# Both parts of x in one product: a two-layer decoder trunk in split fp32 on one core

## The chip, the cores and the metric

The kernel runs on one core of one Trainium2 chip. The metric is device time in microseconds (us), from one launch that computes the whole reference; three runs of the kernel before gave a median of 913.07 us (912.96 to 913.5).

The engines are named as the profile names them: PE is the matrix engine (its weight loads are a row of their own, PEld), DVE the vector engine, ACT the activation engine, POOL the general engine, SP the engine that issues most DMAs.

## The reference, cut to what matters

Two layers, 256 positions, 1024 channels, all in float32. Each layer normalises a mixer's sum and then an MLP's sum:

```
h = layer_norm(x)
for l in range(2):
    h = layer_norm(ALPHA*h + mixer(h))
    gate, val = split(h @ w_up)                 # 2 x 2816 columns
    gate = causal_conv3(gate) + conv_b
    h = layer_norm(ALPHA*h + (silu(gate) * val) @ w_down)
```

The mixer projects h into three groups of heads: A (forgetting attention, `aq`, `ak`, `av`), B (sparse attention with an index of the 64 best keys) and C (differential attention); the three results are gated, added and projected. The units whose products this change rearranges are those of `aq` and `ak`, which the kernel keeps transposed as `qaT` and `kaT`, and the up-projection of the MLP.

## The kernel before, in words

**Split fp32.** Every product is done three times in the matrix engine's fast fp32 form: a value is stored as a high part (`hi`, rounded to that form) and a low part (`lo`, the remainder), and the sum hi·hi + lo·hi + hi·lo is accumulated in a PSUM bank of 128 x 512 floats. Weights come from memory in one flat stream in the order of use (`stream_plan`, L77; class `Stream`, L112): a DMA on SP's queue brings a chunk of 1024 floats per partition into one of 7 `raw` buffers; `Stream.split` (L146) makes an item `hl` of 128 x 2 x 512 in one of 16 buffers, the high part with an ACT copy, the low part with a DVE subtraction (POOL's for some at the start), and then issues the next chunk's DMA on SP.

**Activations.** The normalised h, transposed, is a pair of tiles `hTh` and `hTl` (`new_hT`, L531), each 8 blocks of 128 channels by 256 positions.

**Two kinds of units.** `unit_x` (L668) and `unit_x_tbfirst` (L680) have h as the stationary operand and 512 columns of weights as the moving one, once for each block of 128 positions (`tb`). `unit_w` (L695) has the weights stationary and the 256 positions moving, so that the result comes out transposed. It is used four times for `qaT` and `kaT` (two in each layer) and for pairs 1 to 10 of the MLP in each layer (a pair is 256 gate and 256 value columns; pair 0 goes through `unit_x`'s form and is transposed). For each block k and each of four groups of 128 output columns it issues three products of 128 x 256: wh·xh, wl·xh, wh·xl.

**MLP.** The banks G and V of a pair are handed to `task_act` (L1250): two ACT operations read G (scale and bias of the convolution), four DVE operations read G again (the convolution's other taps), ACT does the silu, DVE multiplies by V, and the result is split into the `act` tile. After the unit of pair j come the 24 products of `down` of pair j-1 into the four `dacc` banks; the products of the last two pairs come at the end, ordered by output half `nh` first and then by pair d, once for each `tb`. `ln_half` (L535) adds the residual and takes statistics of one half.

**The first norm.** `first_norm` (L599), once for each block of 128 positions: h is normalised without gain, transposed by PE into two banks (one for each half q), DVE multiplies each bank by the gain and adds the bias in place (two operations of 128 x 512), and `split_out` (L571) makes the high part with one ACT copy and the low part with one DVE subtraction. `spins(n)` issues n products of no use while PE has nothing to do.

**Order.** Engines run their instructions in the order in which the program emits them. `Clocks` (L201) estimates when each would end, generators (`Tasks`, L282) are advanced at every `T.tick()`, and `refill` (L182) emits splits when the lead in weights is low or DVE has time. `W.hold` stops splits while a norm's chain runs. Banks come from two pools of four: `acc` for the units with h stationary and for `qaT` and `kaT`, `att` for everything else.

Of the kernel before, what the change touches and what calls it, by code (L numbers as in the profile page):

```python
# [76 lines left out]
def stream_plan():  # L77
# [4 lines left out]
    def add(n, kts, cols=512, k0=0):  # L82
        step = 2 if cols <= 512 else 1
        for k in range(k0, k0 + kts, step):
            plan.append((n, k, step, cols))
# [3 lines left out]
    for n in ("biq", "cq", "ck", "cv", "aq", "ak", "av"):  # L89
        add(n, 8)  # L90
    for b in (1, 0):
        for nh in range(2):
            add(f"gate{b}{nh}", 8)
            add(f"br{b}{nh}", 4)
# [10 lines left out]
    for j in range(NPAIR):  # L105
        add(f"up{j}", 8)
# [5 lines left out]
class Stream:  # L112


    def __init__(self, nc, ve, sc, clocks, flat, raw_pool, hl_pool, plan):
# [6 lines left out]
        for (_, _, kts, cols) in plan:  # L122
# [4 lines left out]
            w = 512 if cols >= 512 else cols  # L127
# [68 lines left out]
def part(x):  # L196

    return x.name + "low" if x.name[:2] == "hl" and x.offset % 1024 >= 512 else x.name
# [126 lines left out]
def tile_hybrid(ctx: ExitStack, tc: tile.TileContext, a: dict, out: bass.AP):  # L325
# [273 lines left out]
    def first_norm(tb, st, hT, flag):  # L599
# [13 lines left out]
        for q in range(2):  # L613
# [4 lines left out]
            v = bk.rearrange("p (k t) -> p k t", k=4)  # L618
            for i, f in enumerate((ALU.mult, ALU.add)):
                ve.tensor_tensor(v, v, gb[:, i, 4 * q:4 * q + 4].unsqueeze(2).broadcast_to([P, 4, P]), f)  # L620
        spins((9, 5)[tb])
        if tb:
            att_free(warm)
        for q, bk in enumerate(bks):
            split_out(hT[0][:, 4 * q:4 * q + 4, tb * P:(tb + 1) * P],
                      hT[1][:, 4 * q:4 * q + 4, tb * P:(tb + 1) * P],
                      bk.rearrange("p (k t) -> p k t", k=4))
            att_free(bk)
            if not tb and not q:
                W.split(gp)  # L630
# [64 lines left out]
    def unit_w(hT, bks):  # L695

        for k in range(KD):
            w = W.take()
            for i in range(4):
                o = bks[i // 2][:, (i % 2) * 256:(i % 2) * 256 + 256]  # L700
                l = w[:, :, i * P:(i + 1) * P]
                first = k == 0 and i % 2 == 0
                mm(o, l[:, 0, :], hT[0][:, k, :], first, False)
                mm(o, l[:, 1, :], hT[0][:, k, :], False, False)
                mm(o, l[:, 0, :], hT[1][:, k, :], False, k == KD - 1)
                if i % 2:
                    T.tick()
# [17 lines left out]
    def layer(l, hT, hflag):  # L725
# [524 lines left out]
        def task_act(j, G, V):  # L1250
# [10 lines left out]
            att_free(G)  # L1261
# [3 lines left out]
            att_free(V)  # L1265
# [17 lines left out]
        for j in range(NPAIR):  # L1283
# [3 lines left out]
            G, V = get_att(), get_att()  # L1287
            unit_w(hT1, [G, V])
            T.add(task_act(j, G, V))
# [18 lines left out]
        for tb in range(2):  # L1308
            ts = slice(tb * P, (tb + 1) * P)
            st = small([P, 2, 6], "bst")  # L1310
            for i, (nh, c0, c1) in enumerate(PIECES):
                W.hold = W.hold or nh == 1
                for d in (NPAIR - 2, NPAIR - 1):
                    T.until(lambda: d in acts)
                    for f in range(2):
                        w = ws[d, f, nh][:, :, c0:c1]
                        mm3(dacc[nh][tb][:, c0:c1], acts[d][:, 0, f, ts], acts[d][:, 1, f, ts],
                            w[:, 0, :], w[:, 1, :], False, d == NPAIR - 1 and f == 1)
                        if tb and c1 == 512:
                            W.free()  # L1320
                        if True:
                            T.tick()
                if not (tb and nh and l < DEPTH - 1):
                    ln_half(tb, nh, st, dacc[nh][tb], (c0, c1), i)
# [105 lines left out]
```

## Time and profile before

| | |
|---|---|
| median of 3 runs | 913.07 us (912.96 to 913.5) |
| the profiled execution: time, span | 913.03 us, 911.2 us |
| granted clock of PE, mean | 0.997 |
| PE busy | 898.0 us, 99% of the span, 5334 products |
| PEld busy | 786.7 us, 86% |
| DVE busy | 652.1 us, 72%, 1272 instructions |
| ACT busy | 512.1 us, 56%, 1008 instructions |
| POOL busy | 46.4 us, 5% |
| memory read | 159.47 MB, mean 177 GB/s |

The profile is one execution. Its span runs from the first to the last instruction; the 1.8 us between span and time lie around it. A product's row shows its length in the pipeline, so neighbours overlap: what a product costs in a dense stretch is the distance from one start to the next. All operations have the line of one helper (L276), so rows are told apart by the names of the tiles, written as out<-in.

### The profile page before, as it was taken

The numbers are of one execution on the slowest core, as the hardware profiler recorded it, in microseconds if no ns is written. First come the engines' busy times: TensorE is split into PE (matmuls) and PEld (weight loads), VectorE is DVE, ScalarE is ACT, GpSimd is POOL, SyncE is SP. The second block draws the span as 40 slices with busy tenths as digits, with TensorE's granted clock in tenths as the row PEclk, the third lists the DMA queues.
The fourth block names the chain that finished last, engine by engine and source line by source line (L and its number), as shares of the span: only waits on it lengthen the run. The fifth ranks groups of instructions, "written<-read, shape, count | busy, mean of one in ns | idle before, by whom it ended". The sixth has DMA issues, their size and how long they took to land. (4 is left out here: it accounts for less than half of the span.)

```text
span 911.2 us, 14459 instructions
## 1 busy us (share of the span) xinstructions
PE 898.0 (99%) x5334; PEld 786.7 (86%) x5334; DVE 652.1 (72%) x1272; ACT 512.1 (56%) x1008; POOL 46.4 (5%) x65
## 2 busy tenths in 40 slices
PE   8999999999999999999999999999999999999996
PEld 5878998888888999999888789888888899999995
DVE  6789576966778766666787966775757876766655
ACT  5664766655527555555365556775554475555540
POOL 5100000011010000000000000000200100000000
PEclk9999999999999999999999999999999999999998
DMA  8736253867537665655453335566675376666501
GB/s 300 278 94 205 73 185 116 303 203 242 167 102 273 213 188 182 191 187 177 130 170 137 99 115 162 185 207 211 198 241 183 127 262 188 174 198 187 175 11 47
DMA packets 46680, 161.47 MB, mean 177 GB/s; under 512 B 5840, under 2 KB 6864, under 8 KB 46608
## 3 DMA queue, kind: packets, MB, share of 16 engines
q1 hardware_dynamic: 44208, 155.20, 52.7%
q0 software_dynamic: 1408, 4.98, 2.0%
q8 instruction: 42, 0.69, 0.3%
q10 hardware_dynamic: 992, 0.35, 0.2%
q14 instruction: 30, 0.25, 0.1%
HBM read 159.47 MB, written 1.05 MB: 176 GB/s over the span
## 5 line engine op out<-in xcount | busy, mean ns | idle before, releaser
L276 DVE TENSOR_TENSOR hl<-raw,hl 128x512 fp32r<-128x512 f32 (+1 forms) x580 | 388.4, 695 | 183.3 <-ACT hl L276 181.7
L276 ACT ACTIVATE hl<-raw 128x512 fp32r<-128x512 f32 (+1 forms) x584 | 347.5, 628 | 189.4 <-PE att L276 95.2
L276 PE MATMUL acc<-hl,hTh 128*128 128x512 f32 (+1 forms) x896 | 274.7, 388 | 2.4 <-ACT hTh L276 2.3
L276 PE MATMUL att<-hTh,hl 128*128 128x256 f32 x1280 | 231.5, 283 | 0.0
L276 PEld LDWEIGHTS att<-hTh,hl 128*128 128x128 f32 x1280 | 200.8, 192 | 1.4
L276 PEld LDWEIGHTS acc<-hl,hTh 128*128 128x128 f32 x896 | 166.5, 188 | 38.8 <-ACT hTh L276 4.5
L276 PE MATMUL att<-hTl,hl 128*128 128x256 f32 x640 | 181.1, 283 | 0.0
L276 PE MATMUL acc<-hl,hTl 128*128 128x512 f32 (+1 forms) x448 | 164.8, 385 | 0.1
L276 PE MATMUL acc<-hl,act 128*128 128x512 f32 x528 | 123.1, 390 | 0.0
L276 PEld LDWEIGHTS att<-hTl,hl 128*128 128x128 f32 x640 | 122.8, 192 | 0.0
L276 PEld LDWEIGHTS acc<-hl,act 128*128 128x128 f32 x528 | 98.0, 188 | 19.6
L276 PEld LDWEIGHTS acc<-hl,hTl 128*128 128x128 f32 x448 | 83.9, 188 | 17.0 <-DVE hTl L276 1.8
L276 PE MATMUL acc<-hl,oT 128*128 128x512 f32 x288 | 68.4, 391 | 0.0
L276 PEld LDWEIGHTS acc<-hl,oT 128*128 128x128 f32 x288 | 53.6, 188 | 10.8
L276 DVE SCALAR_TENSOR_TENSOR cv<-att,convp,cv 128x255 f32<-128x255 f32 x88 | 40.4, 479 | 16.1 <-ACT cv L276 14.5
L276 PE MATMUL acc<-hTh,hl 128*128 128x256 f32 x256 | 48.0, 288 | 0.0
L276 PE MATMUL acc<-hl,mT 128*128 128x512 f32 x192 | 44.9, 391 | 0.0
L276 PEld LDWEIGHTS acc<-hl,mT 128*128 128x128 f32 x192 | 35.7, 188 | 7.2
L276 PEld LDWEIGHTS acc<-hTh,hl 128*128 128x128 f32 x256 | 39.8, 191 | 1.5 <-issue 1.3
L276 PE MATMUL acc<-hTl,hl 128*128 128x256 f32 x128 | 36.2, 283 | 0.0
L276 POOL TENSOR_TENSOR rs<-mv,mhalf 128x1 f32<-128x1 f32 x10 | 9.5, 948 | 485.0 <-DVE mv L276 485.0
L276 ACT ACTIVATE t<-acc 128x512 f32<-128x512 f32 (+1 forms) x36 | 20.1, 586 | 21.6 <-PE acc L276 20.8
(166 smaller groups left out, 680.3 us busy)
## 6 DMA issues: line engine op xcount, KB each, us to landing
raw<-in_w_dram SPq DMA_DIRECT2D x284, 512.0 KB, 4.2
raw<-in_w_dram SPq DMA_DIRECT2D x8, 332.0 KB, 4.0
lng<-in_ln_g_dram POOLq DMA_DIRECT2D x4, 512.0 KB, 4.4
lnb<-in_ln_b_dram POOLq DMA_DIRECT2D x4, 512.0 KB, 6.3
h<-in_x_dram SPq DMA_DIRECT2D x4, 256.0 KB, 4.2
lng<-in_ln_in_g_dram SPq DMA_DIRECT2D x1, 512.0 KB, 7.7
lnb<-in_ln_in_b_dram SPq DMA_DIRECT2D x1, 512.0 KB, 8.8
wu<-in_w_ukv_dram POOLq DMA_DIRECT2D x2, 256.0 KB, 5.3
```

The costliest lines, as they stand in the source:

```text
L276: f(*args, **kw)
```

## The change

`new_hT` now makes one tile `hT` in which the high and low parts of a block lie side by side (128 x 8 x 2 x 256), so that both can be the moving operand of one product of 512 columns. `unit_w2` takes the place of `unit_w`: for each block and each of two groups of output columns it issues one product of 512 columns (wh against xh and xl together, into both halves of a bank) and one of 256 (wl against xh, into the first half). A bank so holds one group of 128 output columns, and its halves have to be added. For `qaT` and `kaT` an ACT copy and a DVE multiply-add do that; in the MLP `task_sum` does it, with an ACT copy and a DVE addition for each of the four banks of a pair, into an SBUF tile `gv`, which `task_act` then reads in place of the banks. Weights of these units are streamed as two half matrices of 256 columns, four blocks in a chunk, in the new order of use; the number and size of the chunks stay.

At the end of the MLP the last two pairs are now taken pair by pair and, within a pair, half by half.

In `first_norm` DVE no longer scales the bank in place. For each of the four blocks in a bank ACT writes the high part straight from the bank, with gain and bias as operands, and DVE writes the full value from the same bank into an SBUF tile; one subtraction for each bank then gives the low part. The spins are 3 and 3 where they were 9 and 5; of the three splits with POOL that were emitted before the transposes one now comes after the first bank.

```diff
     def new_hT():
-        return (hp.tile([P, KD, S], R32, name=nm("hTh"), tag="hTh"),
-                hp.tile([P, KD, S], R32, name=nm("hTl"), tag="hTl"))
+        t = hp.tile([P, KD, 2, S], R32, name=nm("hT"), tag="hT")
+        return t[:, :, 0, :], t[:, :, 1, :], t
...
             transpose4(bk, h[tb][q])
-            v = bk.rearrange("p (k t) -> p k t", k=4)
-            for i, f in enumerate((ALU.mult, ALU.add)):
-                ve.tensor_tensor(v, v, gb[:, i, 4 * q:4 * q + 4].unsqueeze(2).broadcast_to([P, 4, P]), f)
-        spins((9, 5)[tb])
+        spins((3, 3)[tb])
...
-            split_out(hT[0][:, 4 * q:4 * q + 4, tb * P:(tb + 1) * P],
-                      hT[1][:, 4 * q:4 * q + 4, tb * P:(tb + 1) * P],
-                      bk.rearrange("p (k t) -> p k t", k=4))
+            full = t2([P, 4, P])
+            for k in range(4):
+                i = 4 * q + k
+                g, b = gb[:, 0, i:i + 1], gb[:, 1, i:i + 1]
+                sc.activation(hT[0][:, i, tb * P:(tb + 1) * P], bk[:, k * P:(k + 1) * P], AF.Identity,
+                              bias=b, scale=g)
+                ve.tensor_scalar(full[:, k, :], bk[:, k * P:(k + 1) * P], g, b, ALU.mult, ALU.add)
             att_free(bk)
+            ks = slice(4 * q, 4 * q + 4)
+            ve.tensor_tensor(hT[1][:, ks, tb * P:(tb + 1) * P], full,
+                             hT[0][:, ks, tb * P:(tb + 1) * P].bitcast(F32), ALU.subtract)
             if not tb and not q:
-                W.split(gp)
+                for _ in range(2):
+                    W.split(gp)
...
-    def unit_w(hT, bks):
+    def unit_w2(hT, bks):
-        for k in range(KD):
+        for k in range(0, KD, 2):
             w = W.take()
-            for i in range(4):
-                o = bks[i // 2][:, (i % 2) * 256:(i % 2) * 256 + 256]
-                l = w[:, :, i * P:(i + 1) * P]
-                first = k == 0 and i % 2 == 0
-                mm(o, l[:, 0, :], hT[0][:, k, :], first, False)
-                mm(o, l[:, 1, :], hT[0][:, k, :], False, False)
-                mm(o, l[:, 0, :], hT[1][:, k, :], False, k == KD - 1)
-                if i % 2:
-                    T.tick()
+            for kk in range(2):
+                for i in range(2):
+                    c = kk * 256 + i * P
+                    mm(bks[i], w[:, 0, c:c + P], hT[2][:, k + kk, :, :], k + kk == 0, False)
+                    mm(bks[i][:, 0:S], w[:, 1, c:c + P], hT[0][:, k + kk, :], False, k + kk == KD - 1)
+                T.tick()
             W.free()
...
-            bks = [acc(), acc()]
-            unit_w(hT, bks)
             t = t4([P, 4, 256])
-            for i in range(2):
-                sc.activation(t[:, 2 * i:2 * i + 2, :], bks[i].rearrange("p (n t) -> p n t", n=2),
-                              AF.Copy, scale=scale)
+            for f in range(2):
+                bks = [acc(), acc()]
+                unit_w2(hT, bks)
+                for i, bk in enumerate(bks):
+                    o = t[:, 2 * f + i, :]
+                    sc.activation(o, bk[:, 0:S], AF.Copy, scale=scale)
+                    ve.scalar_tensor_tensor(o, bk[:, S:], scale, o, ALU.mult, ALU.add)
...
+        def task_pair(j, gv, done):
+            while len(done) < 2:
+                yield
+            yield from task_act(j, gv[:, 0, :], gv[:, 1, :], False)
+
+        def task_sum(gv, f, bks, done):
+            yield from ready("ACT", *bks)
+            for q, bk in enumerate(bks):
+                o = gv[:, q, f * S:f * S + S]
+                sc.activation(o, bk[:, 0:S], AF.Copy)
+                ve.tensor_tensor(o, o, bk[:, S:], ALU.add)
+                att_free(bk)
+            done.append(f)
...
-            G, V = get_att(), get_att()
-            unit_w(hT1, [G, V])
-            T.add(task_act(j, G, V))
+            gv = t4([P, 2, 512], n="gv")
+            done = []
+            for f in range(2):
+                bks = [get_att(), get_att()]
+                unit_w2(hT1, bks)
+                T.add(task_sum(gv, f, bks, done))
+            T.add(task_pair(j, gv, done))
...
-            for i, (nh, c0, c1) in enumerate(PIECES):
-                W.hold = W.hold or nh == 1
-                for d in (NPAIR - 2, NPAIR - 1):
-                    T.until(lambda: d in acts)
+            for d in (NPAIR - 2, NPAIR - 1):
+                T.until(lambda: d in acts)
+                for nh in range(2):
+                    W.hold = W.hold or (nh == 1 and d == NPAIR - 1)
...
     T.tick()
-    for _ in range(3):
+    for _ in range(2):
         W.split(gp)
```

## Rows read from the trace of the kernel before

**Rows 1.** The page: busy time by engine, share of the span, instructions.

```profile
PE 898.0 (99%) x5334; PEld 786.7 (86%) x5334; DVE 652.1 (72%) x1272; ACT 512.1 (56%) x1008; POOL 46.4 (5%) x65
```

**Rows 2.** Timeline, PE, in a pair of the MLP; start, length, count.

```profile
322.06 0.40 PE L276 MATMUL att<-hTh,hl 128*128 128x256 f32 x2
...
322.42 0.40 PE L276 MATMUL att<-hTh,hl 128*128 128x256 f32 x2
```

**Rows 3.** Timeline, PE, the last products into dacc, first layer.

```profile
440.86 16.51 PE L276 MATMUL acc<-hl,act 128*128 128x512 f32 x72
```

**Rows 4.** Groups by form: names, shape, count, busy us, mean ns, idle before.

```profile
L276 PE MATMUL att<-hTh,hl 128*128 128x256 f32 x1280 | 231.5, 283 | 0.0
...
L276 ACT ACTIVATE cv<-att,convp 128x256 f32<-128x256 f32 x44 | 22.5, 562 | 7.9 <-PE att L276 6.3
...
L276 DVE SCALAR_TENSOR_TENSOR h<-h,mv,lng 128x512 f32<-128x512 f32 x16 | 11.2, 744 | 0.0
...
L276 DVE SCALAR_TENSOR_TENSOR h<-h,acc 128x512 f32<-128x512 f32 x16 | 10.9, 682 | 12.4 <-PE acc L276 12.4
...
L276 ACT ACTIVATE oc<-att,rina 128x128 f32<-128x128 f32 x16 | 5.7, 366 | 1.9 <-ACT hl L276 1.4 <-PE att L276 0.5
...
L276 DVE SCALAR_TENSOR_TENSOR oc<-att,crr,dg 128x128 f32<-128x128 f32 x16 | 4.5, 345 | 0.1
...
L276 ACT ACTIVATE kiT<-att 128x256 f32<-128x256 f32 x2 | 0.8, 385 | 0.8 <-PE att L276 0.8
```

**Rows 5.** Windows of 20 us: busy us and count of PE, PEld, DVE, ACT, POOL.

```profile
320.00:340.00 20.00, 20.00 (x148) 19.04 (x146) 12.60 (x21) 10.79 (x18) 0.00 (x0) 1.00 0.60 185
100.00:120.00 20.00, 20.00 (x161) 18.83 (x158) 12.95 (x30) 15.30 (x49) 0.00 (x0) 1.00 0.32 102
```

**Rows 6.** Timeline of the last pair and the end, second layer.

```profile
885.79 1.02 ACT L276 ACTIVATE cv<-att,convp 128x256 f32<-128x256 f32 x2 [4.41 <-PE att L276]
...
886.31 16.51 PE L276 MATMUL acc<-hl,act 128*128 128x512 f32 x72
...
889.51 0.69 DVE L276 TENSOR_TENSOR cv<-cv,att 128x512 f32<-128x512 f32 x1 [0.76 <-ACT cv L276]
890.24 0.63 ACT L276 ACTIVATE act<-cv 128x512 fp32r<-128x512 f32 x1 [0.75 <-DVE cv L276]
890.90 0.69 DVE L276 TENSOR_TENSOR act<-cv,act 128x512 fp32r<-128x512 f32 x1 [0.70 <-ACT act L276]
...
901.96 0.68 DVE L276 SCALAR_TENSOR_TENSOR h<-h,acc 128x512 f32<-128x512 f32 x1
```

**Rows 7.** Timeline around one bank that ACT and then DVE read, second layer.

```profile
489.85 0.69 DVE L276 TENSOR_TENSOR t<-att,t 128x512 fp32r<-128x512 f32 x1 [1.08 <-ACT t L276]
...
490.20 0.39 ACT L276 ACTIVATE kiT<-att 128x256 f32<-128x256 f32 x1 [0.38 <-PE att L276]
...
490.61 0.41 DVE L276 CAST chr<-att 16x256 fp32r<-16x256 f32 x1
```

**Rows 8.** Timeline of the first norm, 0 to 22 us.

```profile
7.00 1.15 ACT L276 ACTIVATE hl<-raw 128x512 fp32r<-128x512 f32 x2 [3.05 <-DMA raw<-in_w_dram]
...
12.01 1.28 DVE L276 BATCH_NORM_STATS2 bst<-h 128x6 f32<-128x512 f32 x2
...
17.25 2.76 DVE L276 TENSOR_TENSOR att<-att,gb 128x512 f32<-128x512 f32 x4 [1.04 <-PE att L276]
```

**Rows 9.** The same, 20 to 42 us: second block, then the second unit.

```profile
20.10 0.60 ACT L276 ACTIVATE hTh<-att 128x512 fp32r<-128x512 f32 x1 [0.73 <-DVE att L276]
...
20.72 1.28 ACT L276 ACT_TABLE_LOAD   x1
...
24.28 3.41 DVE L276 TENSOR_TENSOR hl<-raw,hl 128x332 fp32r<-128x332 f32 x8 [2.85 <-ACT hl L276]
24.43 1.22 PE L276 MATMUL acc<-hl,hTh 128*128 128x512 f32 x5
```

**Rows 10.** One window, hl alone: products on PE, splits on DVE, ACT, POOL.

```profile
0.00:120.00 120.00, 88.41 (x465) 73.23 (x466) 37.91 (x61) 36.46 (x67) 5.01 (x4) 1.00 0.57 191
```

More of the change, by code (lines that the diff above doesn't have):

```diff
@@ L82, in add @@
     def add(n, kts, cols=512, k0=0):
-        step = 2 if cols <= 512 else 1
+        step = {256: 4, 1024: 1}.get(cols, 2)
         for k in range(k0, k0 + kts, step):
@@ L88, in stream_plan @@
     add("g1", 8, NG1)
-    for n in ("biq", "cq", "ck", "cv", "aq", "ak", "av"):
+    for n in ("biq", "cq", "ck", "cv"):
         add(n, 8)
+    for n in ("aq.0", "aq.1", "ak.0", "ak.1"):
+        add(n, 8, 256)
+    add("av", 8)
     for b in (1, 0):
@@ L196, in part @@
 def part(x):
-    return x.name + "low" if x.name[:2] == "hl" and x.offset % 1024 >= 512 else x.name
+    n = {"hl": 1024, "hT": 512}.get(x.name[:2])
+    return x.name + "low" if n and x.offset % n >= n // 2 else x.name
 class Clocks:
@@ L1260, in task_act @@
                 ve.scalar_tensor_tensor(c[:, f, 2:256], g[:, 0:254], cw(f, 0), c[:, f, 2:256], ALU.mult, ALU.add)
-            att_free(G)
+            if banks:
+                att_free(G)
             yield from ready("ACT", c)
@@ L1264, in task_act @@
             ve.tensor_tensor(c, c, V.rearrange("p (f t) -> p f t", f=2), ALU.mult)
-            att_free(V)
+            if banks:
+                att_free(V)
             yield from ready("ACT", c)
@@ L1286, in layer @@
                 continue
-            G, V = get_att(), get_att()
-            unit_w(hT1, [G, V])
-            T.add(task_act(j, G, V))
+            gv = t4([P, 2, 512], n="gv")
+            done = []
+            for f in range(2):
+                bks = [get_att(), get_att()]
+                unit_w2(hT1, bks)
+                T.add(task_sum(gv, f, bks, done))
+            T.add(task_pair(j, gv, done))
             if j in downs and downs[j] and dacc is None:
@@ L1310, in layer @@
             st = small([P, 2, 6], "bst")
-            for i, (nh, c0, c1) in enumerate(PIECES):
-                W.hold = W.hold or nh == 1
-                for d in (NPAIR - 2, NPAIR - 1):
-                    T.until(lambda: d in acts)
+            for d in (NPAIR - 2, NPAIR - 1):
+                T.until(lambda: d in acts)
+                for nh in range(2):
+                    W.hold = W.hold or (nh == 1 and d == NPAIR - 1)
                     for f in range(2):
-                        w = ws[d, f, nh][:, :, c0:c1]
-                        mm3(dacc[nh][tb][:, c0:c1], acts[d][:, 0, f, ts], acts[d][:, 1, f, ts],
+                        w = ws[d, f, nh]
+                        mm3(dacc[nh][tb], acts[d][:, 0, f, ts], acts[d][:, 1, f, ts],
                             w[:, 0, :], w[:, 1, :], False, d == NPAIR - 1 and f == 1)
[L1319 to L1324, printed above, removed]
+                        T.tick()
+                    if d == NPAIR - 1 and not (tb and nh and l < DEPTH - 1):
+                        ln_half(tb, nh, st, dacc[nh][tb])
+                if tb:
+                    W.free(4)
             if l < DEPTH - 1:
@@ L1387, in lay_out @@
                                      w_in[:, OFF["biw"]:OFF["biw"] + 8], w_in[:, OFF["af"]:OFF["af"] + 4]], axis=1)
+        for n in ("aq", "ak"):
+            for f in range(2):
+                mats[f"{n}.{f}"] = mats[n][:, 256 * f:256 * f + 256]
         for nh in range(2):
@@ L1393, in lay_out @@
         for j in range(NPAIR):
-            mats[f"up{j}"] = np.concatenate([inp["w_up"][l][:, 256 * j:256 * j + 256],
-                                             inp["w_up"][l][:, D_FF + 256 * j:D_FF + 256 * j + 256]], axis=1)
+            gate, up = (inp["w_up"][l][:, o + 256 * j:o + 256 * j + 256] for o in (0, D_FF))
+            mats[f"up{j}"] = np.concatenate([gate, up], axis=1)
+            for f in range(2):
+                mats[f"up{j}.{f}"] = np.concatenate([gate[:, P * f:P * f + P], up[:, P * f:P * f + P]], axis=1)
             mats[f"down{j}"] = inp["w_down"][l][256 * j:256 * j + 256, :]
```

9 lines of the change are left out of this document (6 added, 3 removed).

## The prediction

> **What bounds the kernel now.** I read the page's busy times first: PE is busy 898.0 of 911.2 us [rows 1], and its last product ends at 902.8 (886.31 + 16.51) [rows 6]. So PE idles under 5 us in all, and whatever PE's work loses or gains is the kernel's. The second view is PE's own timeline, because busy time cannot tell what one product costs. In a pair of the MLP the starts repeat every 0.36 us for three products of 256 columns, 120 ns each [rows 2]; 72 products of 512 columns in a row take 16.51 us, of which the last is some 0.39, so (16.51 - 0.39)/71 = 227 ns each [rows 3]. Twice the columns cost 107 ns more, not 120: each product carries 13 ns that do not depend on its width. Third, the load on the helpers in the MLP: DVE 12.60 and ACT 10.79 of 20 us [rows 5], so neither is near the bound there. Last, the first norm, where PE does wait for ACT and DVE [rows 8, 9].
>
> **Term 1, the products.** 1280 products of the MLP read hTh and go with half as many that read hTl [rows 4]: 640 triples; the four units for `qaT` and `kaT` have as many for each as a pair has, 32, so 128 more. Each triple of 3 x 120 = 360 ns becomes 227 + 120 = 347. The mixed sequence is not in the trace, but both steps are, and 120 ns already hold a weight load for each product (PEld's count equals PE's [rows 1]), while the new order loads two weights in 347. 768 x 13 = **-10.0 us**. Bounds: 12 to 14 ns, -9.2 to -10.8.
>
> The Trainium skill, page "TensorE: Matmul & The Clock Gate", section "Back-to-back issue gap", gives a warm product N/2.4 + 2.5 ns, so a fixed part of 2.5. Going by it a triple would lose 2.5 ns and the term would be -1.9 us. The trace disagrees for this data type (120 where the Trainium skill has 109, 227 where it has 216), so the rows decide.
>
> **Term 2, sums in the MLP.** Each of 20 pairs gains four ACT copies of 256 columns from a bank (0.385 like kiT) and four DVE additions. DVE's price for 256: 0.682 at 512 columns without a per-partition operand, 0.345 at 128 with one, an operand being 0.744 - 0.682 = 0.062 [rows 4]; that makes 0.283 at 128, a slope of 1.04 ns a column and 0.416 at 256. A pair lasts 32 x 0.360 + 24 x 0.227 = 17.0 us now and 16.6 after. DVE goes from 10.7 to 12.4 us of it (75%), ACT from 9.2 to 10.7 (65%): hidden under PE. Without the cover it would be 3.2 us a pair. Banks: half a pair fills two of four `att` banks and takes 32 x 0.347/2 = 5.6 us, and the additions of the half before end about 1 us into it. The exception is pair 1, beside whose first half pair 0 holds the other two banks: the second half may have to wait for a copy and an addition, 0 to 1.0 us in each layer. I take 0.3 each, since pair 0's banks come free at about that time: **+0.6** (0 to 2).
>
> **Term 3, sums for qaT and kaT.** Two more ACT copies and, new, four DVE operations for each of the four units. They wait for the half's last product, and behind them stand the weight splits and group C's softmax. PE is shielded by the lead in weights, 2.3 items at 120 us (worked out under the rivals), over 3 us. **+0.2** (0 to 2).
>
> **Term 4, the end of the MLP.** The last `act` was ready at 890.90 + 0.69 = 891.59 and needed 24 + 6 products after 886.31, at 893.1 [rows 6]: 1.5 us to spare. Two copies and two additions move its start some 1.5 us later, and taking both halves of pair 9 first (12 products, not 6) moves the need 1.4 us later: still 1.4 to spare. The first half's residual and statistics become due 6 products (1.36 us) before the block's end, not 12. That covers their 1.38 us, and in the second block DVE reaches them only at 901.96 anyway [rows 6]. The hold on splits starts a little later; DVE waited for products then. 0, at worst +0.3.
>
> **Term 5, the first norm.** Here ACT and DVE both read one bank, in the emitted order ACT, DVE, ACT, DVE. The trace shows what that does: DVE was free at 490.54, its cast reads only products long done, in other columns of kiT's bank, and it started at 490.61, 0.02 after ACT's read ended at 490.59 [rows 7]. So DVE waits for ACT's read of a bank although the data have nothing to do with each other. Whether ACT also waits for DVE's read, no row shows.
>
> The Trainium skill, page "PSUM — Partial Sum Buffer", section "PSUM bank collisions raise a hardware error", says that no two engines may be in one bank and partition group at once, reads against reads included. By that the wait goes both ways and the sum is the one below; by the row alone it may go one way, the first rival.
>
> I take both ways: with an order kept between these reads, the next ACT read stands in the same relation to DVE's as DVE's did to ACT's. One of four steps is then: ACT on 128 columns with two per-partition operands, 0.366 with one (oc) + half of 0.562 - 0.385 (cv less kiT) = 0.454; hand-over 0.02; DVE 0.283 + 2 x 0.062 = 0.407; hand-over 0.04 (DVE 890.20 to ACT 890.24 [rows 6]). **0.92 us a step**; bounds 0.77 (one operand less on each) and 1.04 (256 columns: 0.562 and 0.416).
>
> First block: ACT is free at 8.15 [rows 8]. Its fourth read ends at 8.17 + 3 x 0.92 + 0.454 = 11.4; two splits, now placed here, take 1.15 (POOL's halves of them move along, and the DMAs on SP that the splits issue, with seven buffers ahead); the second bank's fourth read ends at 15.8, DVE's at 16.2, the subtraction (0.69) at 16.9. The second block's statistics, next on DVE, so start at 16.9, not 12.01 [rows 8]: 4.9 late. Second block: its first bank is read from 17.25 + 4.9 = 22.15. Fourth ACT read 25.4, DVE's 25.8, subtraction 26.5; ACT's first read of the second bank is done meanwhile, DVE's ends at 26.9, and three more steps put ACT's last at 29.2, where it ended at 20.70 [rows 9]. Behind it on ACT stand the table loads for the sine and then the second unit's weights, whose first item was ready 4.0 us after 20.70 (24.28 + 3.41/8 = 24.71). That makes 33.2 for a unit that began at 24.43 + 4 x 0.227 = 25.34. The other path, the low parts and eight products, gives 32.2. **+7.9 us**. The fewer spins (8 in all) are no gain: PE waits where they stood. Some 12 steps lie on this path, so the bounds of the step are -1.8 and +1.5.
>
> **Sum.** -10.0 + 0.6 + 0.2 + 7.9 = -1.3, made against the profiled execution's 913.03 us (span 911.2 and 1.8 around it), which stands at the median, 913.07. **911.7 us.**
>
> **Rivals.**
>
> *The reads of one bank don't alternate* (ACT runs ahead, DVE follows). For it: only one direction is in the trace. Against it: that direction. ACT's reads are then some 0.35 apart. Fourth read 9.7, splits 10.9, second bank 12.4, subtraction 13.1, statistics 1.1 late; second block from 18.35, last read 21.25, first item 25.26, within 0.1 of now. 913.03 - 10.0 + 0.8 = 903.8.
>
> *Slower: PE runs out of weights in the units for qaT and kaT.* Place: the end of each of the eight halves, where now DVE too stands waiting with the splits behind it. For it: by 120 us 65 low parts were begun (61 DVE, 4 POOL [rows 10]), and of the 465 products 288 belong to six units of 8 items at six products, the rest, at twelve, to 14.75 items, so 62.75 items were used: a lead of 2.3; and ACT is busy 15.30 of 20 us just before [rows 5]. Against it: such a half uses 4 items and the lead is 3 us of products. It decides once the lead at a half's end is under one item; then each half waits for one split (0.58 ACT + 0.69 DVE, 1.3 us): eight halves, 10.4 us, 922.1 us. Already two halves bring it over the time before.
>
> *The product's fixed part doesn't go.* The 13 ns would have to lie elsewhere than in the product, 2.5 in it. Against it are rows 2 and 3. 768 x 2.5 = 1.9 us of gain: 919.8. (The Trainium skill's formula, named under term 1, would make this of it.)
>
> **How the numbers follow.** Forecast case 0.80, no alternation 0.10, weights run out 0.07, fixed part stays 0.03. What this kernel's measurement can tell from no change is about 0.2%, 1.8 us: faster is under 911.2, slower over 914.9. The forecast case's own range is 908.5 to 915.5 (steps -1.8 to +1.5, terms 2 and 3 up to +3.2), and 911.7 lies just inside the upper side of the first limit: I give it 0.32 faster, 0.40 same, 0.08 slower. With 0.10 faster from the first rival and 0.10 slower from the other two: 0.42, 0.40, 0.18. The range is 903.0 to 916.5: to hold 8 in 10 it takes in the first rival and leaves out the last two.
>
> **What would show it.** Term 1: in the MLP starts 227 and 120 ns apart by turns, 32 of each a pair, a pair near 16.6 us, and PE's products 768 fewer. Term 5: on the timeline of the first 35 us ACT's and DVE's 128-column rows by turns, about 0.9 us a pair, statistics of the second block near 17 and the first product of 332 columns near 33. If those reads run side by side and the 332-column unit starts near 25, the first rival holds. Terms 2 and 3: no PE gap over 0.5 us at the halves. I am wrong if the step is far from 0.92, if the tables and splits on ACT fall elsewhere, or if PE's dense stretches show gaps that they lack now.

## The result, and the profile after

The changed kernel takes 925.22 us (median of 4 runs; the kernel before 913.02 beside it): 1.0129 of the time before, 95% interval 1.0117 to 1.0141. That is slower by 12 us, 13.5 us over the forecast and 8.7 over the top of its range. The profiled execution took 926.07 us, the slowest of the four (923.23 to 926.07), with a span of 924.3 us and a mean granted clock of 0.991 (0.997 before). Of all runs below, one is left out of its ratio: one of the eleven of experiment 7, which took 2305.4 us.

The page of after, busy time by engine [rows 1]:

```profile
PE 901.3 (98%) x4558; PEld 748.4 (81%) x4558; DVE 688.0 (74%) x1376; ACT 541.7 (59%) x1108; POOL 46.9 (5%) x65
```

PE runs 776 fewer products (768 joined away, 8 spins), and yet its busy time is 3.3 us longer. The span grew by 13.1. To see where, I took the start of the first product of every unit in both traces. After minus before: 8.3 us at the 332-column unit (the second one), 12.3 at the unit behind it, 13.0 at the first MLP, 12.3 behind it, 13.7 at the second MLP, 13.0 at the end. So nearly all of it is lost in the first 46 us, and after that gains and losses of about one microsecond cancel.

The first norm, timeline of after from 8 us on [rows 8]; start, length, in brackets the idle time before and what ended it:

```profile
8.18 1.15 ACT L284 ACTIVATE hl<-raw 128x512 fp32r<-128x512 f32 x2 [4.23 <-DMA raw<-in_w_dram]
...
9.24 0.44 ACT L284 ACTIVATE hT<-att,gb 128x128 fp32r<-128x128 f32 x1
9.71 0.41 DVE L284 TENSOR_SCALAR t<-att,gb 128x128 f32<-128x128 f32 x1 [2.23 <-ACT hT L284]
...
10.16 0.46 ACT L284 ACTIVATE hT<-att,gb 128x128 fp32r<-128x128 f32 x1 [0.48 <-DVE t L284]
...
10.65 0.41 DVE L284 TENSOR_SCALAR t<-att,gb 128x128 f32<-128x128 f32 x1 [0.53 <-ACT hT L284]
...
16.73 0.41 DVE L284 TENSOR_SCALAR t<-att,gb 128x128 f32<-128x128 f32 x1 [0.53 <-ACT hT L284]
17.17 0.69 DVE L284 TENSOR_TENSOR hT<-t,hT 128x512 fp32r<-128x512 f32 x1
17.78 1.28 DVE L284 BATCH_NORM_STATS2 bst<-h 128x6 f32<-128x512 f32 x2
...
29.70 0.46 ACT L284 ACTIVATE hT<-att,gb 128x128 fp32r<-128x128 f32 x1 [0.48 <-DVE t L284]
30.06 0.47 ACT L284 ACTIVATE hl<-raw 128x332 fp32r<-128x332 f32 x1
...
30.54 1.28 ACT L284 ACT_TABLE_LOAD   x1
...
31.25 0.50 DVE L284 TENSOR_TENSOR hl<-raw,hl 128x332 fp32r<-128x332 f32 x1
```

Each ACT read of the bank ends DVE's wait and each DVE read ends ACT's: a step of 0.94 us with 0.5 of it idle on each engine. The second block's statistics start at 17.78 instead of 12.01.

What follows the norm, from PE's timeline and the one from 30 us on [rows 9]:

```profile
27.52 10.30 PE L284 MATMUL acc<-hl,hT 128*128 128x512 f32 x47 [0.67 <-DVE hT L284]
...
33.59 3.75 ACT L284 ACTIVATE hl<-raw 128x332 fp32r<-128x332 f32 x9
34.11 4.19 DVE L284 TENSOR_TENSOR hl<-raw,hl 128x332 fp32r<-128x332 f32 x9 [2.36 <-ACT hl L284]
...
38.81 0.42 DVE L284 TENSOR_TENSOR ru<-t,cc 128x256 f32<-128x256 f32 x1
...
40.24 1.43 PE L284 MATMUL att<-ident,t 128*128 128x128 f32 x8 [2.42 <-DVE t L284]
```

The 332-column unit starts at 33.61 (25.34 before), inside the row of 47 products, in which PE has no gap. DVE then works off nine low parts before the rope (the rotation by position) of `bq`, and PE waits 2.42 us for it before it can transpose the result. The same two steps before, ACT's splits and the transposes, for which PE did not wait:

```profile
23.77 3.08 ACT L276 ACTIVATE hl<-raw 128x332 fp32r<-128x332 f32 x8
...
29.57 1.06 PE L276 MATMUL att<-ident,t 128*128 128x128 f32 x8
```

Windows of after; the last three columns are granted clock, DMA share, GB/s:

```profile
25.00:30.00 5.00, 3.48 (x8) 2.37 (x9) 2.65 (x6) 2.38 (x6) 1.98 (x6) 0.71 0.78 205
...
35.00:40.00 5.00, 2.82 (x19) 2.55 (x18) 4.96 (x15) 4.86 (x11) 0.00 (x0) 1.00 0.81 244
40.00:45.00 5.00, 4.75 (x23) 4.79 (x24) 4.04 (x8) 3.79 (x7) 0.00 (x0) 0.66 0.99 394
```

Behind PE's idle stretch the granted clock is 0.66 of full speed, that is, a part of these 5 us at the lower of PE's two levels (1.2 and 2.4 GHz). Before the change it was 1.00 there:

```profile
40.00:45.00 5.00, 5.00 (x28) 3.95 (x27) 3.65 (x14) 2.16 (x6) 0.00 (x0) 1.00 0.29 93
```

It had also fallen inside the norm (0.71 from 25 to 30 us), where PE waits again and again.

In the MLP the 64 joined products of a pair stand in one row [rows 2]; the next row is the product behind them:

```profile
329.84 11.45 PE L284 MATMUL att<-hT,hl 128*128 128x512 f32 x64
341.13 0.64 PE L284 MATMUL acc<-hl,act 128*128 128x512 f32 x2
```

From start to start 341.13 - 329.84 = 11.29 us for 32 wide and 32 narrow products, 353 ns for one of each. Before, three products of 120 took 360 (11.51 us for the 96). The single steps are 226 to 241 ns behind a wide product (median 236) and 113 to 120 behind a narrow one (median 117). From pair to pair it is 16.79 us for 16.98 before: of the 0.22 us saved in the joined products, the products of `down` behind them take 0.03 back.

In pair 1 of each layer the second half waits for a bank that pair 0 still holds; timeline of after, first layer:

```profile
301.27 0.64 ACT L284 ACTIVATE gv<-att 128x256 f32<-128x256 f32 x2
301.40 0.69 DVE L284 TENSOR_TENSOR cv<-cv,att 128x512 f32<-128x512 f32 x1 [0.83 <-ACT cv L284]
...
302.14 1.32 PE L284 MATMUL att<-hT,hl 128*128 128x512 f32 x6 [0.97 <-DVE cv L284]
```

### The profile page after: what moved, and what is told of

Read it like the earlier page. It is cut to its first block, busy times and chain, and to the rows that moved or that the text cites. A ratio compares the mean times of both kernels' runs of the same rounds, so it can differ in the third digit from the quotient of the medians.

```text
span 924.3 us, 13132 instructions
## 1 busy us (share of the span) xinstructions
PE 901.3 (98%) x4558; PEld 748.4 (81%) x4558; DVE 688.0 (74%) x1376; ACT 541.7 (59%) x1108; POOL 46.9 (5%) x65
## 5 line engine op out<-in xcount | busy, mean ns | idle before, releaser
L284 PE MATMUL acc<-hl,hT 128*128 128x512 f32 (+1 forms) x1344 | 318.4, 392 | 7.0 <-ACT hT L284 4.0
L284 PEld LDWEIGHTS acc<-hl,hT 128*128 128x128 f32 x1344 | 249.4, 191 | 63.6 <-ACT hT L284 7.3
L284 PE MATMUL att<-hT,hl 128*128 128x512 f32 (+1 forms) x1280 | 230.3, 340 | 1.9 <-DVE cv L284 1.9
L284 PEld LDWEIGHTS att<-hT,hl 128*128 128x128 f32 x1280 | 197.3, 188 | 32.7 <-DVE cv L284 2.6
L284 PEld LDWEIGHTS acc<-hl,oT 128*128 128x128 f32 x288 | 53.5, 188 | 10.8
L284 PE MATMUL acc<-hT,hl 128*128 128x512 f32 (+1 forms) x256 | 49.2, 344 | 0.5 <-DVE hl L284 0.5
L284 PEld LDWEIGHTS acc<-hT,hl 128*128 128x128 f32 x256 | 39.2, 188 | 7.9 <-issue 1.3
L284 ACT ACTIVATE gv<-att 128x256 f32<-128x256 f32 x80 | 29.0, 383 | 21.8 <-PE att L284 21.8
L284 DVE SCALAR_TENSOR_TENSOR cv<-gv,convp,cv 128x255 f32<-128x255 f32 x80 | 36.8, 481 | 1.5
L284 DVE TENSOR_TENSOR gv<-gv,att 128x256 f32<-128x256 f32 x80 | 30.7, 421 | 9.1 <-ACT gv L284 5.2
L284 ACT ACTIVATE t<-acc 128x512 f32<-128x512 f32 (+2 forms) x44 | 20.8, 512 | 15.0 <-PE acc L284 12.2
```

The source lines that it names most:

```text
L284: f(*args, **kw)
```

## The experiments

"The changed kernel" is the one shown above. Each was timed in five rounds beside the kernel before, the last one in one.

**1. The first norm taken back** (`e1_old_norm`), with its spins and the place of its splits; everything else of the change kept:

```
-            full = t2([P, 4, P])
-            for k in range(4):
-                sc.activation(hT[0][...], bk[...], AF.Identity, bias=b, scale=g)
-                ve.tensor_scalar(full[:, k, :], bk[...], g, b, ALU.mult, ALU.add)
+            v = bk.rearrange("p (k t) -> p k t", k=4)
+            for i, f in enumerate((ALU.mult, ALU.add)):
+                ve.tensor_tensor(v, v, gb[:, i, ...], f)
...
+            split_out(hT[0][...], hT[1][...], bk.rearrange("p (k t) -> p k t", k=4))
```

> The changed kernel with the first norm of the kernel before (scale and shift written in place in the bank, then one copy and one subtraction of 512 columns); the joined products and their sums stay. My theory: everything that was lost up to 46 us comes from the first norm (8.3 us up to the first 332-column product, 4.0 more between 33 and 46 us by a fallen clock and a rope that waits behind weight splits), so the 332-column unit starts near 25.3, the next unit near 33.7, and what is left is query/key layer 0 +0.7, MLP -0.7, query/key layer 1 +1.3, MLP -0.65: about 913.7 us, 912.5 to 914.5. Rival: the 4.0 us between 33 and 46 us hang on the new layout of hT or on the changed order of the weight splits and stay: about 917.7.

Measured: 914.43 us, ratio 1.0013 (1.0004 to 1.0022). The 332-column unit starts at 25.56, the next at 33.90; the clock is 1.00 in every window up to 60 us. So the whole loss up to 46 us belongs to the first norm as the change wrote it (reads, spins and splits together), and what is left of the change is a small loss, not the 9 us of gain I had counted for it. The rival is out.

**2. The first norm alone** (`e2_new_norm_only`): the reverse edit in the kernel before.

> The kernel before with the first norm of the changed kernel alone (128-column reads by ACT and DVE in turn, splits moved with it). My theory: 12.3 us are lost by 46 us, 8.3 in the norm and 4.0 behind it, and nothing gives them back: 925.3 us, 924 to 926.5. Rival: only the norm's own delay goes with it, 921.3.

Measured: 926.5 us, ratio 1.0135 (1.0121 to 1.0149). The starts moved by 8.0 and 12.3 us at the same two units and the clock was 0.66 between 40 and 45 us here too (between 25 and 30 us it was 1.00, and still the same 12.3 us were lost):

```profile
40.00:45.00 5.00, 4.76 (x23) 4.79 (x24) 3.62 (x7) 3.46 (x7) 0.00 (x0) 0.66 0.96 388
```

The first norm by itself accounts for the result; its loss neither needs the joined products nor is made good by anything behind it.

**3. The same reads in another order** (`e3_reads_apart`):

```
             for k in range(4):
                 sc.activation(hT[0][:, i, ...], v[:, k, :], AF.Identity, bias=..., scale=...)
+            for k in range(4):
                 ve.tensor_scalar(full[:, k, :], v[:, k, :], ..., ALU.mult, ALU.add)
```

> The changed kernel with the same sixteen pairs of reads in the first norm, the same instructions on the same data, but each bank's four ACT reads stand ahead of its four DVE reads, so that the engine that reads changes once a bank and not seven times. My theory (the reads of one bank keep the order in which they are written, whichever engine they are on): ACT's four reads take some 1.8 us instead of 3.3, DVE's four 1.65 behind them and beside ACT's next bank; the first 332-column product starts near 27 instead of 33.6, 4 to 8 us of the time go, 917 to 921 us. Rival (it is the number of short instructions with their fixed parts that costs, or the position of the splits): the first norm stays within 1.5 us of what it was, 923.5 to 925.5.

Measured: 917.05 us, ratio 1.0041 (1.0029 to 1.0054). Timeline of this kernel, first block:

```profile
9.10 1.49 ACT L284 ACTIVATE hT<-att,gb 128x128 fp32r<-128x128 f32 x4
...
10.62 1.37 DVE L284 TENSOR_SCALAR t<-att,gb 128x128 f32<-128x128 f32 x4 [3.24 <-ACT hT L284]
...
11.51 1.51 ACT L284 ACTIVATE hT<-att,gb 128x128 fp32r<-128x128 f32 x4
```

Four ACT reads take 1.49 us where by turns their starts alone were 2.8 apart (9.24 to 12.04); DVE's first read waits for ACT's last of that bank, while ACT reads the next bank beside DVE. The same instructions, with one change of reader for each bank instead of seven, give 8.2 us back. So the turns cost, not the number of short instructions. At the unit behind the 332-column one 3.8 us of the 12.3 are left; which other part of the new norm takes them was not separated. This shows that the order in which the program writes reads of one bank is kept across engines; whether the chip would mind such reads at the same time, no run here shows.

**4. Wide products first** (`e4_wide_first`), two wide ones and then two narrow ones for each block of weights:

```
-                for i in range(2):
-                    mm(bks[i], w[:, 0, c:c + P], hT[2][...], ...)
-                    mm(bks[i][:, 0:S], w[:, 1, c:c + P], hT[0][...], ...)
+                for i in range(2):
+                    mm(bks[i], w[:, 0, ...], hT[2][...], ...)
+                for i in range(2):
+                    mm(bks[i][:, 0:S], w[:, 1, ...], hT[0][...], ...)
```

> The changed kernel with another order of the joined products: for each row block of weights the two 512-column products (one for each bank), then the two 256-column ones, instead of wide and narrow by turns. In the changed kernel the step from a wide to a narrow product is 236 ns and from a narrow to a wide one 117, 353 a pair of them, 768 pairs. Theory A (the narrow product waits because it adds to columns that the wide one just ahead wrote): steps 227, 227, 120, 120, so 694 for two pairs instead of 706, 6 ns a pair, 4.6 us less: 920.6 us. Theory B (a change of width costs it, whichever bank): half as many changes, 3 ns a pair, 922.9. Theory C (it is the weight load of the narrow product's own weights or the product's own cost): no change, 925.2.

Measured: 920.75 us, ratio 1.0077 (1.0064 to 1.0089); the 64 products of a pair take 11.14 us:

```profile
328.00 11.30 PE L284 MATMUL att<-hT,hl 128*128 128x512 f32 x64
339.14 0.62 PE L284 MATMUL acc<-hl,act 128*128 128x512 f32 x2
```

That is 348 ns for one wide and one narrow, close to the 347 of the forecast. Theory A named this time, but not all that the trace is ahead is its: 1.3 us are there already at the unit behind the 332-column one, where no product of this kind has run yet. In this execution the first weights came sooner, so that ACT's first split starts at 6.96 and not at 8.18, and the norm's last read on ACT ends as much sooner (28.93 for 30.16). From the first joined product to the last product the MLP takes 173.39 us in each layer for 175.17, so the order is worth 3.6 us there, and by estimate 0.6 (128 x 5 ns) for queries and keys.

**5. Narrow products one place later** (`e5_narrow_later`), to tell A from B, on the kernel of experiment 1:

```
                     mm(bks[i], w[:, 0, c:c + P], hT[2][...], ...)
-                    mm(bks[i][:, 0:S], w[:, 1, c:c + P], hT[0][...], ...)
+                    late.append((i, c, k + kk))
+                    if len(late) > 1:
+                        narrow()
...
```

> The changed kernel with the first norm of before, and one more edit: each 256-column product stands one place later, so that it follows the 512-column product of the other bank (within a chunk of four: wide, wide, narrow, wide, narrow, wide, narrow, narrow). With wide products first the pair of the MLP had come down from 11.29 to 11.14 us for half of its products; two causes fit. Theory A (a product that adds to columns which the product just ahead of it wrote starts later): no product does that here, so the half pair falls as far, to 11.14 to 11.17 us, 20 halves of 0.15 and some 0.4 in the query/key stretches: 914.4 - 3.4 = 911.0 us. Theory B (a change of width costs the time): six of eight steps still change width, against eight of eight before and four of eight with wide first, so half as much comes back: 11.22 us, 912.7.

Measured: 913.34 us, ratio 1.0001 (0.9992 to 1.0009). (The text calls 11.29 "half" a pair's products; it is all 64 joined ones. And it says that no product adds to columns which the one just ahead wrote; that holds for the narrow ones, but of the four wide ones in a chunk two now stand right behind the narrow one of their own bank.) A pair's products still take 11.29 us:

```profile
317.42 11.45 PE L284 MATMUL att<-hT,hl 128*128 128x512 f32 x64
328.71 1.31 PE L284 MATMUL acc<-hl,act 128*128 128x512 f32 x5
```

No narrow product follows its own bank's wide one, and the joined products gained nothing. So theory A is out, also when it is taken to hold for the two wide ones, for then half of the gain, 11.22, was due; and the 11.22 of theory B did not come either. The kernel is still 1.1 us faster than that of experiment 1: 0.3 us in each MLP, in the products of `down` behind the joined ones, and the rest in the query and key units.

**6. Pair 0 copied out of its banks** (`e6_pair0_copied`), on the kernel of experiment 1:

```
-            yield from task_act(0, G, V)
+            gv = t4([P, 2, 512], n="gv")
+            yield from ready("ACT", G, V)
+            for q, bk in enumerate((G, V)):
+                sc.activation(gv[:, q, :], bk, AF.Copy)
+                att_free(bk)
+            yield from task_act(0, gv[:, 0, :], gv[:, 1, :], False)
```

> The changed kernel with the first norm of before, and one more edit: pair 0 of the MLP is copied out of its two banks by ACT as soon as its transposes are done (two copies of 512 columns, 1.05 us in each layer), and its convolution and product read the copy. My theory: the second half of pair 1 waits 1.0 us in each layer only because pair 0 holds two of the four banks until its last multiply; with the banks free that stall goes in both layers: 914.4 - 2.0 = 912.4 us. Rival: what the pair waits for is DVE's or ACT's queue, and the copies lengthen it; the stall stays or moves to the next bank: 914.4 or more.

Measured: 911.55 us, ratio 0.9982 (0.9973 to 0.9991), 2.9 us less than experiment 1. Pair 1's stretch falls from 13.40 to 12.16 us in each layer (12.38 before the change) and PE no longer waits in it. The banks were the cause, and the two copies cost nothing.

**7. Queries and keys as before** (`e7_qk_as_before`), with their weights streamed as before; the joined products in the MLP alone, on the kernel of experiment 1:

```
-            for f in range(2):
-                bks = [acc(), acc()]
-                unit_w2(hT, bks)
...
+            bks = [acc(), acc()]
+            unit_w(hT, bks)
```

> The changed kernel with the first norm of before, and the query and key units of the sparse attention taken back to three 256-column products each with plain copies out of the banks; the joined products stay in the MLP alone. My theory: the DVE additions that stand inline in these units, with the softmax and the rope products behind them, cost more than the joined products save there (1.1 us net in layer 0 and 1.3 in layer 1 by the unit starts): 914.4 - 2.4 = 912.0 us. Rival: those shifts are the planner's (another place for the same tasks) and not the additions': the products' 13 - 6 ns come off again as a loss, 914.4 + 0.9 = 915.3 us or no change.

Measured: 911.66 us, ratio 0.9984 (0.9975 to 0.9993), 2.8 us less than experiment 1. In these four units the joined form costs more than it saves.

**8. The first norm of before and three repairs** (`e8_three`): the edits of experiments 1, 4, 6 and 7 together.

> The changed kernel with the first norm of before, wide products first, pair 0 copied out of its banks, and the query and key units as before: the joined products where they pay, without what came with them. If the four causes add up: 914.4 - 3.0 (wide first, 20 half pairs of 0.15) - 2.0 (bank wait) - 2.4 (query and key) = 907.0 us, 906 to 908.5, which is 0.7% under the kernel before. If the repairs overlap or the wait moves, some of it stays: 909 to 911.

Measured: 905.32 us, ratio 0.9913 (0.9899 to 0.9926): faster than both kernels, by 8 us than the one before. The effects add up (914.43 - 3.6 - 2.9 - 2.8 = 905.1). After 20 us no idle stretch of PE over 0.31 us is left.

**9. Four wide, four narrow** (`e9_four_wide`), on the kernel of experiment 8:

```
+            for wide in (True, False):
                 for kk in range(2):
                     for i in range(2):
```

> The kernel with the three repairs, and in each chunk of weights four 512-column products ahead of four 256-column ones, instead of two and two. The step of a product fell only where wide stood by wide and narrow by narrow on the same rows of h (11.14 us for half a pair's products with those of the down projection, against 11.29 by turns and 11.29 with the narrow ones one place later). Theory A (what helps is a neighbour that reads the same rows of h): here each product still has one such neighbour, nothing changes, 905.3 us. Theory B (what costs is the change between wide and narrow): two changes a chunk instead of four, 0.07 us less for each of 20 pairs, 11.07 us, 903.9 us.

Measured: 906.95 us, ratio 0.9932 (0.9919 to 0.9944). A pair's products take 11.20 us, between the two orders, so B (11.07) is out, and A (no change) missed by 1.6 us:

```profile
315.11 11.36 PE L281 MATMUL att<-hT,hl 128*128 128x512 f32 x64
326.31 0.86 PE L281 MATMUL acc<-hl,act 128*128 128x512 f32 x3
```

Why two and two is best stays open.

**10. Sums for queries and keys on POOL** (`e10_qk_sums_pool`), on the kernel of experiment 8:

```
+                r = t4([P, 2, 512], n="qks")
+                for i, bk in enumerate(bks):
+                    sc.activation(r[:, i, :], bk, AF.Copy, scale=scale)
+                gp.tensor_tensor(t[:, 2 * f:2 * f + 2, :], r[:, :, 0:S], r[:, :, S:], ALU.add)
```

> The kernel with the three repairs, but with joined products again for the queries and keys of the sparse attention, wide first, and no work of DVE behind them: ACT copies each bank whole (512 columns, as before the change), and POOL, which stands idle there, adds the two halves from SBUF (eight additions of 512 columns, 1.36 us each by POOL's additions in the first norm). Theory (what the change lost there came from DVE's additions, which stand in its queue until the half's last product, with splits and softmax behind them): nothing waits, the products bring 128 x 11 ns = 1.4 us: 903.9 us. Rival (the shifts come from the half units, shorter units with a bank change each, or from the order in which the tasks then fall): 1.1 and 1.3 us of shift come back, less 1.4 for the products, 905.3 to 907.5 us.

Measured: 910.13 us, ratio 0.9967 (0.9955 to 0.9979), 4.8 us more than experiment 8. My theory falls: with no addition on DVE the four units still lose 1.1 us in layer 1 (1.3 in experiment 1), and in layer 0 they lose 3.6 (1.1). Timeline of this kernel in the first half of the key unit, layer 0:

```profile
109.04 0.48 ACT L284 ACTIVATE a<-att,smx 128x256 f32<-128x256 f32 x1 [1.44 <-DVE smx L284]
...
111.53 0.69 DVE L284 TENSOR_TENSOR hl<-raw,hl 128x512 fp32r<-128x512 f32 x1 [1.92 <-ACT hl L284]
111.55 2.40 PE L284 MATMUL acc<-hT,hl 128*128 128x512 f32 x10 [1.09 <-ACT hl L284]
...
114.45 0.39 PE L284 MATMUL acc<-hT,hl 128*128 128x256 f32 x1 [0.51 <-DVE hl L284]
```

Here PE runs out of split weights: a split stands behind a softmax that ACT could not start before DVE's maximum. This is the wait of my second rival, in the middle of a half. Which part of the loss comes from the shorter units and which from the order in which tasks then fall was not separated.

**11. PE kept busy where it waits for the rope** (`e11_rope_spins`), on the changed kernel:

```
                 bk = yield from att()
+                if key == "qbT" and not l and not tb:
+                    for _ in range(10):
+                        mm(bk, spin, spin.unsqueeze(1).broadcast_to([P, 4, P]), True)
                 transpose4(bk, s[:, tb, :])
```

> The changed kernel with ten products of ones put ahead of the transposes of bq (the place at 37.5 to 40.2 us where PE waits for DVE's rope), into the bank that the transposes then write; nothing else. Theory (the granted clock of 0.66 between 40 and 45 us follows from PE's idle 2.4 us there): the clock stays at 1.00 in 40 to 45, the unit after the 332-column one starts 10.6 us after it instead of 12.3, and the kernel takes 923.5 us. Rival (it follows from PE's many waits before, from 20 to 30 us, or the spins delay the transposes): the clock falls all the same, 12.3 us or more, 925.2 us.

Measured: 923.5 us (2 runs), ratio 1.0112 (1.0093 to 1.013). That time alone shows little, as the changed kernel itself took 923.23 to 926.07; the trace does. Windows of this kernel:

```profile
25.00:30.00 5.00, 3.89 (x10) 2.87 (x10) 2.88 (x7) 2.84 (x7) 1.29 (x4) 0.66 1.00 197
30.00:35.00 5.00, 5.00 (x28) 4.45 (x28) 2.64 (x7) 4.96 (x11) 1.57 (x7) 1.00 0.65 198
35.00:40.00 5.00, 4.87 (x30) 3.35 (x30) 4.96 (x14) 3.99 (x9) 0.00 (x0) 1.00 0.78 263
40.00:45.00 5.00, 5.00 (x33) 4.77 (x31) 4.14 (x7) 4.92 (x12) 0.00 (x0) 1.00 1.02 399
```

The clock stays at 1.00 from 30 us on, although it is 0.66 between 25 and 30, and the stretch from the 332-column unit to the next falls from 12.30 to 10.59 us. So of the 4.0 us lost behind the norm the clock took 1.7, and the idle 2.4 us were what lowered it; the other 2.3 are the wait for the rope. The other traces agree: with a gap of 2.4 us there (the changed kernel, experiments 2 and 4) the clock in 40 to 45 us is 0.66, 0.66 and 0.70, without one (experiment 3) 1.00.

## Why the prediction was wrong

Four terms came out worse than forecast and none better. The two large misses are the steps that failed: the end of term 5 (12.3 us for 7.9) and the size of term 1 (-4.7 us for -10.0).

**The end of term 5** is "That makes 33.2 for a unit that began at 24.43 + 4 x 0.227 = 25.34", whose difference, +7.9, the sum then takes as what the norm costs the kernel. Of the norm itself the forecast was right: the reads go by turns both ways, the step is 0.94 us against 0.92, and from the first split's end on ACT (9.33) to its last read's end (30.16) it takes 20.8 us against 21.05. Behind it two things went otherwise.

First, that the unit starts at 33.61, near 33.2, is luck. The forecast let it wait for weights behind the table loads on ACT. But one split of these weights stood ahead of the table loads, at 30.06, and its low part was done at 31.75; PE came to the unit when it was through with the first unit's products. In experiment 2, where the clock was 1.00, that was at 33.34, eight products behind the last low part of h (31.33): the path that the forecast had at 32.2 and took for the one that ends sooner. The number came near because the norm began late, as ACT's first split waited for its DMA until 8.18 (7.00 before). That is about one microsecond of the 12.3: in the trace of experiment 4, where that split starts at 6.96, the unit behind the 332-column one is 11.0 us late. The norm of before hid such a delay almost wholly (experiment 1: split at 8.01, 332-column unit at 25.56).

Second, the unit's first product is not where the delay ends. ACT's other splits of these weights do stand behind the table loads. They start 9.8 us later than before (33.59 for 23.77), DVE's low parts and the rope follow them, and the transposes that need the rope start 10.7 us later (40.24 for 29.57). Before, the 27 products of the 332-column unit that stand ahead of the transposes just covered that wait; now PE idled 2.4 us, the granted clock fell behind it, and the next unit is 12.3 us late, 4.4 more than the term (experiments 1, 2 and 11). The question "what is late next" was asked of the unit's first product, and not of the transposes, whose wait for DVE had lost its cover.

The terms, each with what it measured:

- Term 1, -10.0. The step behind a wide product is 236 ns and not the 227 it had among its like; behind a narrow one it is 117, not 120. So 353 for 347, and 7 ns saved for 13. With what the products of `down` take back, it is 20 pairs x 0.19 us and, by estimate, 128 x 7 ns: -4.7 us, outside its bounds of -9.2 to -10.8. I had taken a mixed sequence as the sum of two plain ones. The order matters (11.14, 11.20 and 11.29 us for the same 64 products), for a reason that I did not find.
- Term 2, +0.6. The place was right and the size above what I took: pair 1 took 1.24 us more in each layer than without the wait (experiment 6), +2.5, where the bounds ended at 2 for both layers. "Pair 0's banks come free at about that time" was the choice that failed; they came free at 302.1, a microsecond late. The sums of the other pairs are hidden, as said: DVE 421 and ACT 383 ns each, for 416 and 385 forecast, and no PE gap.
- Term 3, +0.2. By the unit starts the four units lost 0.7 us in layer 0 and 1.3 in layer 1, net of the 0.9 that their products saved (counted in term 1), so the term is +3.0. Experiment 7 gave 2.8 back from experiment 1, where the net loss was 1.1 and 1.3. The lead in weights was no shield. In layer 1 PE waited 1.50 us for DVE's copy of `q`, which stood behind the addition and two low parts (timeline of after):

```profile
562.36 0.76 DVE L284 SCALAR_TENSOR_TENSOR t<-acc,t 128x256 f32<-128x256 f32 x2 [2.20 <-ACT t L284]
...
563.64 1.29 DVE L284 TENSOR_TENSOR hl<-raw,hl 128x512 fp32r<-128x512 f32 x2 [0.53 <-ACT hl L284]
...
564.85 0.68 DVE L284 COPY q<-att 128x512 f32<-128x512 f32 x1
...
565.68 2.63 PE L284 MATMUL att<-q,vb 128*128 128x256 f32 x14 [1.50 <-DVE q L284]
```

  In layer 0 PE waited for split weights, 0.23 us twice in the changed kernel and 1.0 us in experiment 1, from whose page this group is:

```profile
L284 PE MATMUL acc<-hT,hl 128*128 128x512 f32 (+1 forms) x256 | 49.6, 345 | 1.0 <-ACT hl L284 0.8
```

  That the additions are the cause is not shown (experiment 10), only that the joined form of these units is.
- Term 4, 0: right. The last 48 products take 11.04 us in both kernels and the end behind them moved by 0.04.

With the measured sizes, -4.7 + 2.5 + 3.0 + 12.3 = 13.1, the 13.1 by which the span of the profiled execution grew (the medians lie 12.2 apart). With 12.3 for term 5 and all else as forecast the sum would have been 916.1, inside the range, and with -4.7 for term 1 alone 917.0, just outside; it took four errors on one side to leave the range by 8.7 us. The forecast case's own upper end was added up wrongly (911.7 + 1.5 + 3.2 is 916.4, not 915.5), which alters nothing here.

Of the rivals, the one without turns is refuted by the rows of the norm. The one with a fixed part that stays is half true: 7 of 13 ns went. The slower one named the right units and its wait is there, but it reckoned with 1.3 us at each of eight halves: experiment 1 has one such wait, 0.79 us at the first product of the key unit in layer 0, where a half has just ended.

## What to carry to other kernels

When a step at the start becomes late, follow the delay past the next unit, along each engine's queue to the last product that waits for it: the work that hid other waits no longer covers them, and PE's idle time may be paid again in clock. A number that comes out right at one point says little until the wait that ended there is the one that was forecast. Two engines that read one bank should each finish their reads before the other begins, or read different banks. And a saving per product that is put together from two plain sequences should carry the mixed sequence's uncertainty, as the order alone moved it by 5 ns of 353.

## What the runs showed of the hardware

- Products of 512 and 256 columns by turns do not cost the sum of their plain steps: 353 ns a couple, 348 in groups of two, 350 in groups of four, 353 with the narrow ones shifted, against 227 + 120 = 347. Neither the bank written just before nor the number of changes of width explains the four numbers. The Trainium skill, page "TensorE: Matmul & The Clock Gate", section "Back-to-back issue gap", gives a formula for a warm product by itself, N/2.4 + 2.5 ns, by which a couple would take (512 + 256)/2.4 + 2 x 2.5 = 325 ns, an estimate that no order of these products came near.
- PE's idle 2.4 us between 37.8 and 40.2 us were followed by a granted clock of 0.66 from 40 to 45 us; ten products of no use in that place kept it at 1.00 and were worth 1.7 us.
- ACT reads of 128 columns with two operands start 0.34 us apart in a row (four rows of 0.44 to 0.46 us overlap to 1.49) and 0.94 us apart by turns with DVE.
- The first weights, whose DMA is issued at 1.65 us in every trace, let ACT's first split start between 6.69 and 8.20 us. With the norm by turns all that follows shifts as much (experiment 4: 1.2 us sooner at the split, 1.3 at the unit behind the 332-column one).
